# Two low rank products issued as a pair, and the state products of two heads alternated in two banks, in a two-layer hybrid decoder trunk

## The chip, the core and the metric

The kernel runs on one core of one Trainium2 chip. The metric is the device time of one execution in microseconds (us), median of several runs; lower is better. The program uses five engines with a queue of instructions each: TensorE (PE, with its weight loads as PEld), VectorE (DVE), ScalarE (ACT), GpSimd (POOL) and SyncE (SP, which issues most transfers). Products land in PSUM, which this kernel cuts into eight banks of 128 x 512 float32.

## What is computed

Two layers, 1024 tokens, width 1024, float32. Only layer 0's mixer and one function of layer 1 are touched by the change.

```python
# layer 0: y = concat(rwkv7(x), gla(x)) @ w_out ; layer 1: y = concat(s5(x), hgrn2(x)) @ w_out
# each layer: x = LN(alpha*x + mixer(x)); x = LN(alpha*x + hierarchical_moe(x))   (32 experts, top 2)
def rwkv7(p):                       # 8 heads of 64
    w = -softplus(-(w0 + tanh(wl) @ w2)) - 0.5      # low rank product 1: the decay
    a = sigmoid(a0 + al @ a2)                       # low rank product 2: the gate a
    kk = normalize(k * k_k)
    k = k * (1 + (a - 1) * k_a)
    S_t = S * exp(-exp(w)) + (S @ -kk) (kk * a)^T + v k^T ;  y_t = S_t r_t
    y = (groupnorm(y) + bonus) * (sigmoid(gl) @ g2) # low rank product 3
def gla(q, k, v, g):                # 4 heads, 64 x 128 states; hgrn2: 4 heads, 128 x 128
    o = q_decayed @ S_chunk  +  scores @ v          # a product with the state, one with the scores
```

## The kernel before

Everything is emitted by one Python program for the Tile framework; a scheduler then sets the order of each engine's queue. A queue runs in that order. What the scheduler may move is bounded by data and by buffers: a name such as `po` stands for a ring of PSUM banks (`RINGS`, line 654; `po` is the single bank f, `pp` the single bank e, `y` bank g, `ch` bank h, `iv` and `gs` the two banks c and d), and the users of a ring take it in the order in which the program text asks for it. A product into a ring of one bank waits until the last reader of the bank's former content, in the order of the text, is through.

Layer 0 (`layer0`, L1692) does two blocks of 512 tokens, n = 0 and 1. In each, `rwkv` (L282) runs four halves (`rwkv_half`, L314), one per pair of heads, pr = 0 to 3. For each half three projections are made (`proj_T`: L175, L176, L177, 24 products each into bank ring `pj`). Then `gla` (L607) makes its projections and runs `gla_core` (L512) twice, for two heads each. `gla` reuses buffers of `rwkv` by name.

One RWKV half is a long chain:

- the first low rank product (L328) and its sigmoid give the decay `cum`, `P`; the second (L340) and its sigmoid give `av`, from which DVE makes `k`, `av*kk` and the four parts of `BK` (L354 to L365);
- transposes of `BK` (L398), scores (L408), masks on DVE (L412 to L414);
- the inverse of a triangular matrix by doubling: nine groups of 16 small products (L425), each read by DVE (L433, L435, L440) before the next;
- a recurrence over 8 chunks: three products per chunk in ring `ch` (L447, L452, L458) with copies by ACT (L450, L454) and DVE (L453, L461) between them, and the output products (L466, L467);
- the tail: three products into `po` (group norm L471 and L475, third low rank product L482), then `y*p` on DVE (L483), the last reader of `po`.

Each half asks for `pp` and `po` in this order: `pp` for both low rank products and two more (L346, L369), `po` for the tail's three.

`gla_core` ends with the products of each head in turn: for each of four chunks one with the state (L571) and one with the scores (L572) into one bank of ring `y`, which before held the sums for the new states (L562), read by DVE (L566). Layer 1 calls `gla_core` with one head of 128 rows (`hgrn2_head`, L1303).

Of the kernel before, what the change touches and what calls it, by code (L numbers as in the profile page):

```python
# [35 lines left out]
class Kern:  # L36
# [38 lines left out]
    def store(self, dst, src):  # L75
        self.nc.gpsimd.dma_start(dst, src)
# [233 lines left out]
    def work(self, name, shape=(128, 512), bufs=1):  # L310
        tag, bufs = self.tags.get(name, (name, bufs))
        return self.place.get(tag, self.mpool).tile(list(shape), F32, tag=tag, bufs=bufs, name=name)

    def rwkv_half(self, pr, n, k, r_, v, wlal, sgl, ydram):  # L314
        nc, K, work = self.nc, self.rk, self.work
        C, lora = K["C"], K["lora"]
        cs = slice(pr * 128, (pr + 1) * 128)
# [3 lines left out]
        def col(i):  # L321
            return C[:, i + pr:i + pr + 1]

        def c8(x):
            return x.rearrange("p (c t) -> p c t", t=64)


        p = self.mm1(lora[0:64, 0, cs], wlal[0:64])  # L328
        sg = work("sg")
        self.sigmoid(sg, p, bias=col(14))  # L330
        cum = work("cum")
        nc.vector.tensor_tensor_scan(cum, self.cmask.rearrange("p c t -> p (c t)"), sg, 0.0, op0=OP.mult, op1=OP.add)
# [3 lines left out]
        nc.scalar.activation(iP, cum, AF.Exp, scale=EC)  # L336
        PC = work("PC", (128, 8), bufs=2)
        nc.gpsimd.tensor_copy(PC, c8(P)[:, :, 63])

        p = self.mm1(lora[64:128, 0, cs], wlal[64:128])  # L340
        av = work("av")
        self.sigmoid(av, p, bias=col(18))

        sq = work("tmp", bufs=2)
        nc.scalar.activation(sq, k, AF.Square, scale=col(22))
        p = self.mm1(self.blk, sq)  # L346
# [10 lines left out]
        Q, Zd = self.pairs[pr % 2]  # L357
        BK = work("BK", (128, 8, 2, 64))
        for h in range(2):
            r = H[h]  # L360
# [8 lines left out]
        p = self.mm1(self.blk, r_)  # L369
# [32 lines left out]
        for g in range(2):  # L402

            sc = [piv().rearrange("p (c x) t -> p c x t", x=2) for _ in H]
            for j in range(4):
                c = 4 * g + j
                for h, r in enumerate(H):
                    nc.tensor.matmul(sc[h][:, j], BK[r, c], Q[r, c, 2 * h:2 * h + 2, :], start=True, stop=True)  # L408
            for h, psc in enumerate(sc):
                r, rk = H[h], H[1 - h]  # L410
# [10 lines left out]
        def diag(lhs, rhs):  # L421
            p = piv()
            for j in range(8):
                for r in H:
                    nc.tensor.matmul(p[r, j, :], lhs[r, j, :], rhs[r, j, :], start=True, stop=True)  # L425
            return p
# [4 lines left out]
        for s in (2, 4, 8, 16, 32):  # L431
# [5 lines left out]
            else:  # L437
                p = diag(T1, Z)
# [5 lines left out]
        y = work("y")  # L444
        for c in range(8):
# [16 lines left out]
            if c % 4 == 3:  # L462
                py = self.bank("y", (128, 4, 2, 64))
                for j in range(4):
                    i = c - 3 + j
# [5 lines left out]
        p = self.mm1(self.blk, y, "po")  # L471
# [3 lines left out]
        p = self.mm1(self.blk, sq, "po")  # L475
# [6 lines left out]
        p = self.mm1(lora[:, 1, cs], sgl, "po")  # L482
# [29 lines left out]
    def gla_core(self, n, q, k, f, heads, S, norm_g, store):  # L512

        nc, work = self.nc, self.work


        SC = [work(f"gSC{i}", (128, 4, 128), bufs=2) for i in range(len(heads))]
        Q, Ke, D = work("gQ", bufs=2), work("gK", bufs=2), work("gD")
        nc.vector.tensor_tensor(Q, q, f, op=OP.mult)
        d, at = f, 0  # L520
        for s in (0, 1, 2, 4, 8, 16, 32, 64):
            L, R = (k if s < 2 else Ke), Q if s else q
            ps = [self.bank("gs", (128, 4, 128)) for _ in heads]
            if s:
                ps = [p.rearrange("p (h c) t -> p h (c t)", h=2)[:, 0].rearrange("p (c t) -> p c t", t=64) for p in ps]
            for c in range(4):
                cc = slice(128 * c, 128 * c + 128)
                for p, (r, _, _, _) in zip(ps, heads):
                    rhs = R[r, cc]
                    if s:  # L530
                        rhs = rhs.rearrange("p (b t) -> p b t", t=2 * s)[:, :, s:]
                    if s < 64:
                        nc.tensor.matmul(p[:, c, :], L[r, cc], rhs, start=True, stop=True)  # L533
                    else:
                        nc.tensor.matmul(p[0:64, c, :], L[r, 128 * c:128 * c + 64], rhs, start=True, stop=True)
            if s:
                nb = 256 // s
                b3 = lambda x: x.rearrange("p (b t) -> p b t", t=2 * s)
                d2 = d.rearrange("p (b h) -> p b h", h=2)
                bc = lambda h: d2[:, :, h:h + 1].to_broadcast([128, nb, s])  # L540
                if s == 1:
                    nc.gpsimd.tensor_copy(b3(Ke)[:, :, 1:], b3(k)[:, :, 1:])
                nc.vector.tensor_tensor(b3(Ke)[:, :, :s], b3(L)[:, :, :s], bc(1), op=OP.mult)
                nc.vector.tensor_tensor(b3(Q)[:, :, s:], b3(Q)[:, :, s:], bc(0), op=OP.mult)
                d = D[:, at:at + nb]
                at += nb
                nc.vector.tensor_tensor(d, d2[:, :, 0], d2[:, :, 1], op=OP.mult)
            for i, p in enumerate(ps):
                if s == 64:
                    nc.scalar.activation(SC[i][0:64, :, 64:], p[0:64], AF.Copy)  # L550
                elif s == 0:
                    nc.vector.tensor_tensor(SC[i], p, self.ident[:, None, :].to_broadcast([128, 4, 128]), op=OP.mult)
                else:
                    m = self.glev[s].rearrange("p (b t) -> p b t", t=s)[:, None].to_broadcast([128, 4, 64 // s, s])
                    nc.vector.copy_predicated(SC[i].rearrange("p c (b t) -> p c b t", t=2 * s)[:, :, :, s:], m,
                                              p.rearrange("p c (b t) -> p c b t", t=s))
        kdT = self.token_major(Ke, "gkdT")

        pS = self.bank("y", (128, 4, 128))
        for c in range(4):  # L560
            for r, V, _, _ in heads:
                nc.tensor.matmul(pS[r, c, :], kdT[:, c, r], V[:, c, :], start=True, stop=True)  # L562
        St = work("gS", (128, 4, 128), bufs=2)
        for c in range(4):
            src = S if c == 0 else St[:, c - 1, :]
            nc.vector.scalar_tensor_tensor(St[:, c, :], src, d[:, c:c + 1], pS[:, c, :], op0=OP.mult, op1=OP.add)  # L566
        for i, (r, V, gate, row) in enumerate(heads):
            po = self.bank("y", (128, 4, 128))
            for c in range(4):
                cc = slice(128 * c, 128 * c + 128)  # L570
                nc.tensor.matmul(po[:, c, :], S[r, :] if c == 0 else St[r, c - 1, :], Q[r, cc], start=True, stop=False)  # L571
                nc.tensor.matmul(po[:, c, :], V[:, c, :], SC[i][:, c, :], start=False, stop=True)  # L572
            o = work("go", bufs=2)
            nc.scalar.activation(o, po.rearrange("p c t -> p (c t)"), AF.Copy)
            sq = work("ptmp")
            nc.scalar.activation(sq, o, AF.Square)
            p = self.mm1(self.ones, sq, "po")
            nc.scalar.activation(sq, p, AF.Ln, scale=1.0 / 128, bias=self.eps)
            nc.scalar.activation(sq, sq, AF.Exp, scale=-0.5)
            nc.vector.scalar_tensor_tensor(o, o, norm_g, sq, op0=OP.mult, op1=OP.mult)  # L580
            store(row, o, gate)
        nc.gpsimd.tensor_copy(S, St[:, 3, :])
# [1211 lines left out]
```

## Time and profile before

| | |
|---|---|
| median of 3 runs | 2887.45 us (2884.76 to 2890.49) |
| the profiled execution's own time | 2887.3 us |
| its span | 2885.5 us |
| granted TensorE clock over the span | 0.951 of full |
| layer 0's mixer, first to last product | about 0 to 800 us of the span |
| layer 0's experts | about 900 to 1500 us |
| layer 1's mixer | about 1550 to 2150 us |
| layer 1's experts | about 2200 to 2830 us |

The profile is one execution. Its span leaves out 1.8 us of the execution's own time. A row of the timeline gives the start, the duration, the engine and the instruction (a product of float32 shows as two records, marked x2). A row of a table by stretch gives the busy time of each engine in it, with the number of instructions, then the granted clock, the share of the DMA engines, and GB/s.

### The profile page before, as it was taken

What the parts mean: (1) busy time and instruction counts of PE and PEld (TensorE: products, weight loads), DVE (VectorE), ACT (ScalarE), POOL (GpSimd) and SP (SyncE); (2) the same over time, 40 slices, a digit from 0 to 9 for tenths busy, and PEclk for the clock granted to TensorE, in tenths of its full rate; (3) what the DMA queues carried; (4) which work ended last, traced back from release to release, by engine and by line L of the source; (5) the groups of instructions that cost most, each with busy time, mean ns of one, the idle gap of its engine ahead of it and who ended that gap; (6) DMA issues with size and microseconds to landing.
All of it is one profiled execution on the core that took longest, in us unless ns stands there. A gap on an engine that the chain in (4) does not pass through costs nothing.

```text
span 2885.5 us, 41351 instructions
## 1 busy us (share of the span) xinstructions
PE 2670.9 (93%) x15348; PEld 1980.4 (69%) x15348; DVE 2100.3 (73%) x3228; ACT 1586.0 (55%) x2292; POOL 819.5 (28%) x991
## 2 busy tenths in 40 slices
PE   8999999999897999999988788789997999999994
PEld 6777776766685677777764667678776677777772
DVE  5775447764357899999967568886445899999985
ACT  4343333333333788888864333334533788888872
POOL 5333323323400211111105455462320111111104
PEclk9999989999897999999999889899898999999998
DMA  3111221101354999999967221122443999999985
GB/s 112 31 38 34 62 74 38 30 28 48 128 174 178 373 379 378 378 376 380 385 250 232 88 62 45 56 67 77 140 150 134 355 379 381 382 382 378 380 309 191
DMA packets 234644, 581.57 MB, mean 202 GB/s; under 512 B 48110, under 2 KB 156743, under 8 KB 185287
## 3 DMA queue, kind: packets, MB, share of 16 engines
q1 hardware_dynamic: 212294, 518.04, 50.1%
q0 software_dynamic: 22144, 60.85, 6.0%
q8 instruction: 122, 2.00, 0.3%
q14 instruction: 84, 0.68, 0.1%
HBM read 541.99 MB, written 52.43 MB: 206 GB/s over the span
## 4 chain that ended last, share of the span: by engine, by line
issue 36%; PE 32%; DVE 10%; POOL 8%; DMA 2%; ACT 2%; POOLq 0%; SPq 0%; DVEq 0%; ACTq 0%
POOL xg L970 4%; PE bpj L176 4%; PE bpj L177 4%; PE bpj L175 4%; PE bgs L533 3%; POOL ybuf L1034 2%; PE bpj L729 2%; PE bpj L730 2%; PE bpj L728 2%; PE biv L425 1%; PE bpp L785 1%; PE bpo L182 1%; PE biv L1220 1%; PE by L571 1%; PE by L572 1%
## 5 line engine op out<-in xcount | busy, mean ns | idle before, releaser
L111 DVE TENSOR_TENSOR mlo<-raw,mhi 128x1024 fp32r<-128x1024 f32 x768 | 921.8, 1222 | 105.4 <-ACT mhi L1058 71.2
L1058 ACT ACTIVATE mhi<-raw 128x1024 fp32r<-128x1024 f32 x768 | 806.4, 1059 | 204.5 <-PE bpo L1027 87.1
L118 POOL TENSOR_TENSOR wlo<-wraw,whi 128x256 fp32r<-128x256 f32 x368 | 282.4, 797 | 323.0 <-ACT whi L106 309.3
L175 PE MATMUL bpj<-hT_hi,whi 128*128 128x512 f32 x736 | 306.2, 416 | 12.7 <-DVE hq L588 11.8
L970 POOL DMA_INDIRECT xg<-hdram,gi x64 | 135.4, 2116 | 632.0 <-PE by L982 600.9
L177 PE MATMUL bpj<-hT_hi,wlo 128*128 128x512 f32 x736 | 305.1, 415 | 4.5 <-POOL wlo L118 4.5
L176 PE MATMUL bpj<-hT_lo,whi 128*128 128x512 f32 x736 | 306.4, 416 | 0.0
L996 PE MATMUL bpj<-mhi,xh 128*96 128x512 f32 x512 | 204.9, 400 | 0.0
L106 ACT ACTIVATE whi<-wraw 128x1024 fp32r<-128x1024 f32 x92 | 97.3, 1057 | 195.4 <-PE bpj L176 140.7
L998 PE MATMUL bpj<-mhi,xl 128*96 128x512 f32 x512 | 204.4, 399 | 0.1
L997 PE MATMUL bpj<-mlo,xh 128*96 128x512 f32 x512 | 204.0, 399 | 0.0
L996 PE MATMUL biv<-mhi,xh 128*96 128x512 f32 x512 | 201.8, 394 | 0.0
L997 PE MATMUL biv<-mlo,xh 128*96 128x512 f32 x512 | 201.6, 394 | 0.0
L998 PE MATMUL biv<-mhi,xl 128*96 128x512 f32 x512 | 201.6, 394 | 0.0
L175 PEld LDWEIGHTS bpj<-hT_hi,whi 128*128 128x128 f32 x736 | 142.5, 194 | 47.0 <-DVE hq L588 13.1
L1034 POOL DMA_INDIRECT ybuf<-yo,si x64 | 60.2, 940 | 385.1 <-ACT yo L1033 375.4
L177 PEld LDWEIGHTS bpj<-hT_hi,wlo 128*128 128x128 f32 x736 | 142.0, 193 | 34.8 <-POOL wlo L118 6.7
L176 PEld LDWEIGHTS bpj<-hT_lo,whi 128*128 128x128 f32 x736 | 142.0, 193 | 30.0 <-issue 3.8
L998 PEld LDWEIGHTS bpj<-mhi,xl 128*96 128x96 f32 x512 | 84.1, 164 | 38.0 <-DVE xl L111 1.4
L729 PE MATMUL bpj<-wol,oyh 128*128 128x512 f32 x256 | 105.8, 413 | 4.2 <-POOL wol L118 4.2
L997 PEld LDWEIGHTS bpj<-mlo,xh 128*96 128x96 f32 x512 | 84.2, 164 | 36.5 <-issue 0.2
L996 PEld LDWEIGHTS bpj<-mhi,xh 128*96 128x96 f32 x512 | 84.1, 164 | 35.9 <-issue 0.2
(617 smaller groups left out, 5686.7 us busy)
## 6 DMA issues: line engine op xcount, KB each, us to landing
raw<-in_moe_w_dram SPq DMA_DIRECT2D x384, 1024.0 KB
wraw<-in_ab_w_in_dram SPq DMA_DIRECT2D x50, 512.0 KB
wraw<-in_cd_w_in_dram SPq DMA_DIRECT2D x40, 512.0 KB
cy<-ybuf SPq DMA_DIRECT2D x16, 1024.0 KB
oyr<-ydram SPq DMA_DIRECT2D x16, 512.0 KB
hdram<-or POOLq DMA_DIRECT2D x16, 512.0 KB, 2.9
lnh<-hdram SPq DMA_DIRECT2D x16, 512.0 KB
ydram<-go POOLq DMA_DIRECT2D x16, 256.0 KB, 2.7
```

The lines of the kernel that those rows point to most:

```text
L111: self.keep(self.nc.vector.tensor_tensor(lo, src, hi.bitcast(F32), op=OP.subtract))
L118: lo_engine.tensor_tensor(lo[:, s], src[:, s], hi[:, s].bitcast(F32), op=OP.subtract)
L175: nc.tensor.matmul(dst, wh[:, k, :], xh[:, k, :], start=(k == 0), stop=False)
L176: nc.tensor.matmul(dst, wh[:, k, :], xl[:, k, :], start=False, stop=False)
L177: nc.tensor.matmul(dst, wl[:, k, :], xh[:, k, :], start=False, stop=(k == KT - 1))
L729: nc.tensor.matmul(p, yh[:, k, :], wl[:, ds_], start=False, stop=False)
L970: self.nc.gpsimd.indirect_dma_start(out=xg[:CAP, :], out_offset=None, in_=hdram, in_offset=bass.IndirectOffsetOnAxis(ap=gidx, axis=0), bou ...
L996: self.keep(self.nc.tensor.matmul(p, xh[:, k, :], wh, start=(k == 0), stop=False))
L997: self.keep(self.nc.tensor.matmul(p, xh[:, k, :], wl, start=False, stop=False))
L998: self.keep(self.nc.tensor.matmul(p, xl[:, k, :], wh, start=False, stop=(k == KT - 1)))
L1034: return nc.gpsimd.indirect_dma_start(out=ybuf, out_offset=bass.IndirectOffsetOnAxis(ap=sidx, axis=0), in_=y, in_offset=None, bounds_check ...
L1058: self.keep(self.nc.scalar.activation(hi, src, AF.Copy))
```

## The change

1. In `rwkv_half` the second low rank product is issued right after the first one, in the text, and lands in ring `po` in place of `pp`. Its sigmoid stays where it was.
2. In `gla_core` the products with the states come first, for both heads alternating by chunk, head 0 in ring `y` and head 1 in ring `ch`; the products with the scores follow head by head. The bank is opened once (start on the first chunk alone).

```diff
-        p = self.mm1(lora[0:64, 0, cs], wlal[0:64])
-        sg = work("sg")
+        p, pa = self.mm1(lora[0:64, 0, cs], wlal[0:64]), self.mm1(lora[64:128, 0, cs], wlal[64:128], "po")
+        sg, av = work("sg"), work("av")
         self.sigmoid(sg, p, bias=col(14))
...
-
-        p = self.mm1(lora[64:128, 0, cs], wlal[64:128])
-        av = work("av")
-        self.sigmoid(av, p, bias=col(18))
+        self.sigmoid(av, pa, bias=col(18))
...
-        for i, (r, V, gate, row) in enumerate(heads):
-            po = self.bank("y", (128, 4, 128))
+
+        pos = [self.bank(x, (128, 4, 128)) for x in ("y", "ch")[:len(heads)]]
+        for c in range(4):
+            for po, (r, _, _, _) in zip(pos, heads):
+                nc.tensor.matmul(po[:, c, :], S[r, :] if c == 0 else St[r, c - 1, :], Q[r, 128 * c:128 * c + 128], start=(c == 0), stop=False)
+        for i, (po, (r, V, gate, row)) in enumerate(zip(pos, heads)):
             for c in range(4):
-                cc = slice(128 * c, 128 * c + 128)
-                nc.tensor.matmul(po[:, c, :], S[r, :] if c == 0 else St[r, c - 1, :], Q[r, cc], start=True, stop=False)
-                nc.tensor.matmul(po[:, c, :], V[:, c, :], SC[i][:, c, :], start=False, stop=True)
+                nc.tensor.matmul(po[:, c, :], V[:, c, :], SC[i][:, c, :], start=False, stop=(c == 3))
```

What it does to the order of PE's queue, at three places. In these rows a b ahead of a ring's name marks its bank, and from L344 to L558 a line of the changed kernel is 3 less than the same line before.

The first place is PE around the end of the half pr = 1 and the start of pr = 2, first block. Before:

```order
L182 MATMUL bpo<-ptmp,blk 128x512
L425 MATMUL biv<-T_1387,Z 64x64 x16
L182 MATMUL bpp<-wlal,lora 128x512
L182 MATMUL bpo<-sgl,lora 128x512
L425 MATMUL biv<-X,M 64x64 x16
L175 MATMUL bpj<-hT_hi,whi 128x512
L176 MATMUL bpj<-hT_lo,whi 128x512
L177 MATMUL bpj<-hT_hi,wlo 128x512
L175 MATMUL bpj<-hT_hi,whi 128x512
L182 MATMUL bpp<-wlal,lora 128x512
```

And with the change:

```order
L182 MATMUL bpo<-y,blk 128x512
L182 MATMUL bpo<-ptmp,blk 128x512
L182 MATMUL bpo<-sgl,lora 128x512
L182 MATMUL bpo<-wlal,lora 128x512
L395 MATMUL biv<-ident,BK 128x64 x14
L182 MATMUL bpp<-r,blk 128x512
L395 MATMUL biv<-ident,BK 128x64 x2
L405 MATMUL biv<-Q_275,BK 128x128 x8
L182 MATMUL bpp<-wlal,lora 128x512
```

The rows before are the tail of pr = 0 (`bpo`), the inverse of pr = 1 (L425) and both low rank products of pr = 2 (`wlal,lora`). The rows after are the tail of pr = 1, then the second low rank product of pr = 2, its transposes (L395, before L398) and scores (L405, before L408), and the first low rank product of pr = 3. The second product of a half now stands behind the tail of the half ahead of it; in the half pr = 0 of each block alone the two stand side by side.

The second place is PE in the recurrence of pr = 1, first block, two chunks of the eight. Before:

```order
L447 MATMUL bch<-SV,Q_281 128x128
L425 MATMUL biv<-X,M 64x64 x8
L452 MATMUL bch<-G,Zd_282 128x64
L425 MATMUL biv<-X,M 64x64 x5
L175 MATMUL bpj<-hT_hi,whi 128x512
L176 MATMUL bpj<-hT_lo,whi 128x512
L177 MATMUL bpj<-hT_hi,wlo 128x512
L458 MATMUL bch<-UV,BT 128x128
L466 MATMUL by<-R_1267,UV 128x128
L467 MATMUL by<-Q_281,SV 128x128
L425 MATMUL biv<-T_1957,Z 64x64 x3
```

And with the change:

```order
L444 MATMUL bch<-SV,Q_281 128x128
L449 MATMUL bch<-G,Zd_282 128x64
L455 MATMUL bch<-UV,BT 128x128
L463 MATMUL by<-R_1267,UV 128x128
L464 MATMUL by<-Q_281,SV 128x128
L444 MATMUL bch<-SV,Q_281 128x128
L449 MATMUL bch<-G,Zd_282 128x64
L455 MATMUL bch<-UV,BT 128x128
```

Before, the next half's inverse and projections stand between the products of the recurrence. Now nothing does, from its fourth chunk to its end, and all through that of pr = 2.

The third place is PE at the end of `gla_core`, first block, first two heads. Before, head 0:

```order
L571 MATMUL by<-gQ,glS 128x128
L572 MATMUL by<-gSC_3190,gV 128x128
L571 MATMUL by<-gQ,gS 128x128
L572 MATMUL by<-gSC_3190,gV 128x128
L571 MATMUL by<-gQ,gS 128x128
L572 MATMUL by<-gSC_3190,gV 128x128
```

And with the change, both heads:

```order
L568 MATMUL bch<-gQ,gS 128x128
L571 MATMUL bch<-gSC_3191,gV 128x128 x2
L568 MATMUL by<-gQ,glS 128x128
L568 MATMUL by<-gQ,gS 128x128 x3
L571 MATMUL by<-gSC_3190,gV 128x128 x4
L571 MATMUL bch<-gSC_3191,gV 128x128 x2
```

The four state products of head 1 (`bch`) go ahead one by one, the last of them in the first row here, and those of head 0 (`by`) follow in one run, when bank g is free. The two heads do not alternate in the queue.

In layer 1 the only difference is that the four products with the state stand ahead of the four with the scores, in each of the eight calls; from layer 0's experts on all else stands as before.

## Rows read from the trace of the kernel before

**Rows 1.** The page, busy time of each engine, share of the span:
```profile
PE 2670.9 (93%) x15348; PEld 1980.4 (69%) x15348; DVE 2100.3 (73%) x3228; ACT 1586.0 (55%) x2292; POOL 819.5 (28%) x991
```

**Rows 2.** Busy time by stretch (columns: PE, PEld, DVE, ACT, POOL, clock, DMA):
```profile
143.00:306.00 163.00, 160.48 (x1509) 112.84 (x1508) 103.11 (x219) 62.62 (x147) 56.34 (x92) 1.00 0.13 38
306.00:366.00 60.00, 59.49 (x348) 44.41 (x347) 26.90 (x54) 20.19 (x33) 20.23 (x27) 0.97 0.22 67
...
527.00:691.00 164.00, 160.95 (x1526) 113.73 (x1524) 103.77 (x214) 64.53 (x150) 56.35 (x90) 1.00 0.12 35
```

**Rows 3.** Timeline of PE: second low rank product of pr 1; last tail products:
```profile
84.55 0.69 PE L182 MATMUL bpp<-wlal,lora 64*128 64x512 f32 x1
...
143.24 0.70 PE L182 MATMUL bpo<-sgl,lora 128*128 128x512 f32 x1
...
196.34 0.70 PE L182 MATMUL bpo<-sgl,lora 128*128 128x512 f32 x1
...
305.39 0.70 PE L182 MATMUL bpo<-sgl,lora 128*128 128x512 f32 x1
...
526.70 0.70 PE L182 MATMUL bpo<-sgl,lora 128*128 128x512 f32 x1
...
691.08 0.70 PE L182 MATMUL bpo<-sgl,lora 128*128 128x512 f32 x1 [0.38 <-ACT ptmp L477]
```

**Rows 4.** Timeline of DVE and ACT: last reader of po; from av to the inverse:
```profile
146.90 0.68 DVE L483 TENSOR_TENSOR y<-y,bpo 128x512 f32<-128x512 f32 x1
...
434.70 0.75 DVE L191 TENSOR_SCALAR av<-bpp,rwp 128x512 f32<-128x512 f32 x1 [0.35 <-PE bpp L182]
...
435.48 0.63 ACT L192 ACTIVATE av<-av 128x512 f32<-128x512 f32 x1 [0.45 <-DVE av L191]
...
448.85 0.69 DVE L365 TENSOR_TENSOR BK<-k,cum 64x512 f32<-64x512 f32 x1
...
462.60 0.70 DVE L430 STREAM_TRANSPOSE X<-Z 128x512 f32<-128x512 f32 x1
```

**Rows 5.** Timeline: one step of the inverse, PE to DVE to PE:
```profile
90.96 1.15 PE L425 MATMUL biv<-T,Z 64*64 64x64 f32 x32
...
92.40 0.68 DVE L435 TENSOR_TENSOR X<-X,biv 128x512 f32<-128x512 f32 x1
...
93.39 1.15 PE L425 MATMUL biv<-X,M 64*64 64x64 f32 x32
```

**Rows 6.** Timeline of PE: the recurrence, from one chunk's first product to the next's:
```profile
277.58 0.46 PE L447 MATMUL bch<-SV,Q 128*128 128x128 f32 x2
...
280.91 0.46 PE L447 MATMUL bch<-SV,Q 128*128 128x128 f32 x2
```

**Rows 7.** Timeline of PE: the recurrence's last output product, first product of the tail:
```profile
299.39 0.39 PE L467 MATMUL by<-Q,SV 128*128 128x128 f32 x2
...
300.64 1.12 PE L182 MATMUL bpo<-y,blk 128*128 128x512 f32 x2
```

**Rows 8.** A stretch, and the same 16 records (8 products) at either clock:
```profile
380.00:390.00 10.00, 8.85 (x51) 7.54 (x51) 6.69 (x14) 2.71 (x4) 4.42 (x6) 0.50 0.39 107
...
372.70 2.85 PE L533 MATMUL bgs<-gQ,gK 64*128 64x64 f32 x16 [0.33 <-DVE gQ L544]
...
327.83 1.11 PE L533 MATMUL bgs<-gQ,gK 64*128 64x64 f32 x16
```

**Rows 9.** Timeline of PE: state and score products in turn; state-like products of two heads alternating:
```profile
336.48 0.48 PE L571 MATMUL by<-gQ,glS 64*128 64x128 f32 x2
336.89 0.49 PE L572 MATMUL by<-gSC,gV 128*128 128x128 f32 x2
...
306.45 1.16 PE L533 MATMUL bgs<-gq,gk 64*128 64x128 f32 x14
```

**Rows 10.** Timeline of PE: two projection products, start to start:
```profile
43.87 0.39 PE L177 MATMUL bpj<-hT_hi,wlo 128*128 128x512 f32 x1
44.09 0.39 PE L175 MATMUL bpj<-hT_hi,whi 128*128 128x512 f32 x1
```

## The prediction

> **What bounds the kernel now.** I read the busy shares first, then the table by stretch, then PE's timeline of one RWKV half, and last the queue orders printed above. PE is busy for 93% of the span [rows 1]. In layer 0's mixer it is more than that: 160.48 of 163 us over the halves pr = 1 to 3 of the first block, 160.95 of 164 us in the second [rows 2]. DVE, the next, has a third of that time free. So layer 0's mixer is bound by PE, and it is so only because the halves overlap: the second low rank product of pr = 1 runs at 84.55 us, long before the tail of pr = 0 ends with its third product at 143.24 us [rows 3]. While one half's recurrence goes from engine to engine, PE works on the next half's inverse. From tail to tail a half takes (305.39 - 143.24) / 3 = 54.0 us in the first block and (691.08 - 526.70) / 3 = 54.8 us in the second [rows 3].
>
> **The change, part by part.** *The low rank pair.* The second product moves from ring pp to ring po. In the program's text the uses of po by the half ahead (its tail) come first, so the product must wait until that tail's last reader, y*p on DVE, is through. Behind it wait av, k, BK, the transposes, scores, inverse and recurrence of its own half. The order shows it: three tail products, then this one, then the transposes; and the recurrences of pr = 1 and 2 stand alone in the queue. Three of the four halves of a block thus become one serial chain from tail to tail. Its length, from rows:
>
> - third tail product to the end of y*p: 143.24 to 146.90 + 0.68, so 4.4 us [rows 3, 4];
> - the second low rank product: 1.2 us, as the tail's first product of the same width (1.12) and a handoff [rows 7];
> - from it to the end of BK: one DVE step of 0.75, three ACT steps of 0.63, seven DVE steps of at most 0.69, with handoffs about 7.6 us [rows 4];
> - end of BK (448.85 + 0.69) to the end of the transpose that opens the inverse (462.60 + 0.70): 13.8 us, some of it other halves' work; I take 13.0 [rows 4];
> - nine steps of the inverse at 93.39 - 90.96 = 2.43 us: 21.9 us, the last one's DVE work standing for the step to the recurrence [rows 5];
> - eight chunks at 280.91 - 277.58 = 3.33 us: 26.6 us [rows 6];
> - last output product to third tail product: 305.39 - 299.39 = 6.0 us [rows 3, 7].
>
> The sum is 80.7 us against 54.0 and 54.8: 26.7 and 25.9 us more per half, 80 and 78 us per block for its three halves.
>
> *The clock.* Where PE has few and small products the granted clock has fallen to half, 1.2 of 2.4 GHz: in 380 to 390 us it is 0.50, and the same 8 products take 2.85 us there against 1.11 [rows 8]. The bare recurrences offer PE three dependent products of about 0.46 us per 3.33 us [rows 6]. No row shows one at half clock. The bounds are nothing, and a doubling of every product on the chain. I take 6 us for pr = 1 (five bare chunks and the tail), 16 for pr = 2 (eight chunks, the bare steps of its inverse, its tail), and 4 for pr = 3, whose recurrence shares PE and DVE with the first gla_core: 26 us per block, about half of the upper bound, which I put at 52.
>
> *What comes back.* The first half of a block loses work that the order moves behind its tail: by count 64 inverse products (4 groups of 1.15 us), three products of 1.12 us and 32 transposes and scores (4 us at 1.11 per 8), and gains 23 projections at 0.22 us [rows 5, 7, 8, 10]: 6 us earlier. And the scheduler fills pr = 3 with the first gla_core: between its tail and the second gla_core stand 100 projections and no gK products, where before 144 projections and 63 such products filled 60 us at 99% PE [rows 2]. 44 projections are 10 us [rows 10]; 63 products at 1.11 per 8 and some switching 11 us [rows 8]; the transposes, a product of 1.12 us and the state products below the rest: 27 us. Per block: 80 + 26 - 6 - 27 = 73 and 78 + 26 - 6 - 27 = 71 us. Sum: 144 us.
>
> *The state products.* Before, a state product of 64 rows and a score product of 128 rows start 0.41 us apart, while 14 records (7 products) on the two halves of the rows, alternating, take 1.16 us in all [rows 9]. Alternated, 8 state products would cost 1.3 us in place of 3.3, and with the scores in runs the 16 products about 3.3 us in place of 6.7. The order does not alternate them: ring y still holds the sums for the states, so head 1 goes ahead alone and head 0 follows. What is left is fewer changes of shape, about 2 us a call; two calls are inside the 27 above, the two others give 4 us. The Trainium skill, in TensorEngine Tiling (Array Packing), section Tiling Modes, says that tiles of different rows run in parallel and that a change of the tiling mode drains the engine. Rows 9 agree with both. By that rule with full alternation in all four calls and all eight pairs this change would be a gain; that is a rival below.
>
> *Layer 1.* Here both products have 128 rows. Four state products run ahead of four score products, so up to three of the latter no longer cover DVE's state updates: at most 3 x 0.41 us [rows 9] in eight calls, 10 us, least 0. PE is not the bound there throughout; I take 2. The experts move as they are.
>
> **The sum.** 144 - 4 + 2 = 142 us, onto the profiled execution's own 2887.3 us (0.15 below the median): **3029 us**.
>
> **The rivals.**
> - *The clock stays up.* Full clock in the bare stretches takes off 2 x 26 us: 2977. For it: three products per chunk and projections between most inverse steps. Against: the half clock in 380 to 390 us, where PE was nominally busy for 8.85 of 10 us [rows 8].
> - *Half clock all through the serial halves,* and the first gla_core crowding pr = 3's recurrence: twice the surcharge, 52 us more, and half of the 27 us lost in both blocks, 27 more: 3108. The Trainium skill, in TensorE: Matmul & The Clock Gate, Part 1, says that a gate passes half of the clock's pulses or all by how busy PE has been; it is on the side of a low clock here, and the sum does not use it.
> - *Faster: PE stays the bound.* If po were free in time, or projections filled the waits, only the savings would stay: two pairs side by side at one product each (2 x 1.2 us) and 4 x 2 us: 2877; with all pairs and states overlapped, 8 x 1.2 + 4 x 3.4 = 23 us: 2864. It decides from the point where a serial half fits into 54 us, or where the projections at hand fill the rest. Against: the order has 24 projections, 5 us, in the whole period of pr = 2, and 80.7 is far from 54.
> - *The delay is hidden by other work,* say because DMA-bound stages after it absorb some: 2930. Little speaks for it; the stages after start from layer 0's last output.
>
> **How the numbers follow.** The forecast, 3029 with half of the clock's surcharge, has 0.64; full clock 0.15; half clock throughout 0.15; partly hidden 0.02; faster 0.03; no change 0.01. The range runs from 2972, a little under the full clock case, to 3090, into the low clock case, whose upper part is left out with the faster and hidden ones. Faster and slower mean by over 0.2% (5.8 us), about what a measurement of this kernel can tell. Slower has 0.64 + 0.15 + 0.15 + 0.02 = 0.96.
>
> **What would show it.** In the changed profile: the second low rank product of pr = 1 to 3 some 5 us behind the third tail product of the half ahead; 80 to 100 us from tail to tail for these halves; PE busy for about half of the period of pr = 2 and the clock at 0.5 in the bare recurrences; the second gla_core of the first block starting near 437 us in place of 366; stages after layer 0 of the same length. It is wrong if halves still overlap, if tail to tail stays under 65 us, or if the expert stages change.

## The result, and the profile after

The changed kernel takes **3040.27 us** (median of 4 runs, 3039.48 to 3041.52) against 2888.52 us (2884.76 to 2890.49) for the kernel before on the same chip: a ratio of 1.0522, 95% interval 1.051 to 1.0535. The forecast was 3029, slower. The profiled execution took 3041.52 us, 154.2 us more than that of before; its span is 3039.7 us, its mean granted clock 0.913 against 0.951.

The page of the changed kernel, the busy time of each engine and the slices of PE and its clock:

```profile
PE 2734.0 (90%) x15348; PEld 2023.8 (67%) x15348; DVE 2109.1 (69%) x3228; ACT 1583.4 (52%) x2292; POOL 807.6 (27%) x991
...
PE   8986899987899889999998887889999699999995
...
PEclk8977898986899889999999988989989799999997
```

and the same two rows of slices of the kernel before:

```profile
PE   8999999999897999999988788789997999999994
...
PEclk9999989999897999999999889899898999999998
```

The work is the same, the instruction counts too [rows 1]. PE's busy time has grown by 63 us, with not one product more: the same products at a lower clock. The slices that have fallen are in the first third, layer 0's mixer.

PE's timeline of the changed kernel shows where (start, duration, instruction, what ended the idle time before it):

```profile
135.77 1.13 PE L182 MATMUL bpo<-sgl,lora 128*128 128x512 f32 x2
140.13 1.12 PE L182 MATMUL bpo<-wlal,lora 64*128 64x512 f32 x2
...
226.75 2.08 PE L182 MATMUL bpo<-sgl,lora 128*128 128x512 f32 x2 [0.78 <-ACT ptmp L474]
230.23 2.07 PE L182 MATMUL bpo<-wlal,lora 64*128 64x512 f32 x2 [1.41 <-DVE y L480]
...
317.29 2.08 PE L182 MATMUL bpo<-sgl,lora 128*128 128x512 f32 x2 [0.78 <-ACT ptmp L474]
320.77 2.07 PE L182 MATMUL bpo<-wlal,lora 64*128 64x512 f32 x2 [1.41 <-DVE y L480]
...
406.76 1.02 PE L182 MATMUL bpo<-sgl,lora 128*128 128x512 f32 x2
...
439.61 1.16 PE L530 MATMUL bgs<-gq,gk 64*128 64x128 f32 x16
...
592.63 1.12 PE L182 MATMUL bpo<-sgl,lora 128*128 128x512 f32 x2
...
863.83 1.02 PE L182 MATMUL bpo<-sgl,lora 128*128 128x512 f32 x2
...
896.68 1.16 PE L530 MATMUL bgs<-gq,gk 64*128 64x128 f32 x16
```

Read the pairs. `sgl,lora` is the tail's third product of one half, `wlal,lora` into `bpo` the second low rank product of the next. Each follows the tail by 3.5 to 4.4 us, and the idle time before the second and third ends with `DVE y L480`: y*p, the last reader of `po`. Before, that product ran at 84.55 us for pr = 1, a whole tail ahead [rows 3]. From tail to tail it is now 91.0, 90.5 and 89.5 us, where it was 54.0 [rows 3]. `bgs<-gq,gk` opens the second `gla_core`: it stands 32.9 us behind the last tail in either block, where it was 60 and 57.6 us before.

The same by stretch (PE, PEld, DVE, ACT, POOL, clock, DMA share, GB/s):

```profile
136.00:227.00 91.00, 77.24 (x608) 53.59 (x608) 44.22 (x86) 25.28 (x56) 26.88 (x42) 0.81 0.12 33
227.00:317.00 90.00, 62.01 (x518) 42.51 (x518) 38.63 (x79) 19.20 (x48) 11.89 (x24) 0.67 0.03 10
317.00:407.00 90.00, 83.81 (x721) 61.17 (x722) 53.86 (x114) 29.21 (x65) 19.63 (x32) 0.93 0.12 33
407.00:440.00 33.00, 33.00 (x166) 24.72 (x166) 13.12 (x23) 12.74 (x20) 11.87 (x19) 1.00 0.27 89
```

Before, these halves had PE busy for 160.48 of 163 us at clock 1.00 [rows 2]. No engine is near its limit now in the period of pr = 2: PE 62 of 90 us (with products stretched by the clock), DVE 39. That is what a chain looks like.

### The profile page after: what moved, and what is told of

It is laid out like the page before. It is cut to its first block, busy times and chain, and to the rows that moved or that the text cites. A ratio compares the mean times of both kernels' runs of the same rounds, so it can differ in the third digit from the quotient of the medians.

```text
span 3039.7 us, 41356 instructions
## 1 busy us (share of the span) xinstructions
PE 2734.0 (90%) x15348; PEld 2023.8 (67%) x15348; DVE 2109.1 (69%) x3228; ACT 1583.4 (52%) x2292; POOL 807.6 (27%) x991
## 4 chain that ended last, share of the span: by engine, by line
issue 34%; PE 24%; DVE 8%; POOL 8%; ACT 2%; DMA 2%; POOLq 0%; SPq 0%; DVEq 0%; ACTq 0%
POOL xg L969 4%; PE bpj L175 2%; PE bpj L177 2%; PE bpj L176 2%; PE bgs L530 2%; POOL ybuf L1033 2%; PE bpj L728 2%; PE bpj L727 2%; PE bpj L729 2%; PE bpp L784 1%; POOL wol L118 1%; PE bpo L182 1%; PE biv L1219 1%; PE biv L422 1%; DVE sX L1588 1%
## 5 line engine op out<-in xcount | busy, mean ns | idle before, releaser
L530 PE MATMUL bgs<-gQ,gK 64*128 64x64 f32 (+1 forms) x640 | 87.3, 319 | 24.7 <-DVE gQ L541 23.8
```

## Experiments

**1. The low rank pair alone.** The diff is the first half of the change, as printed above (`pa` in ring `po`); `gla_core` is that of before.

> The kernel before with the low rank pair alone (second product early in the text, in ring po); gla_core as before. Theory A (the one bank of po makes three halves of each block serial): nearly all of the 152 us, 3025 to 3045 us; tails some 90 us apart; layer 1 as before. Rival B (the state products ahead of the score products cost a good part): under 2990 us.

Measured: 3049.88 us (3042.92 to 3050.8) against 2889.28; ratio 1.0547 [1.0517, 1.0578]. Its stretches from tail to tail read as those of the whole change:

```profile
136.00:227.00 91.00, 76.71 (x610) 52.69 (x609) 44.80 (x87) 25.72 (x56) 26.90 (x42) 0.83 0.12 33
227.00:318.00 91.00, 64.80 (x519) 45.08 (x518) 38.31 (x79) 19.29 (x48) 11.89 (x24) 0.61 0.03 10
```

The pair carries all of the loss. The time lies 5 us above the expected range, about what the states, which are missing here, gain in run 2.

**2. The state products alone.** The second half of the change, on the kernel before.

> The kernel before with the state products alone moved; low rank products as before. Theory A: 2880 to 2900 us, a few us gained in layer 0's two blocks by fewer changes of shape and some 4 us lost in layer 1, where no score product covers DVE's state updates. Rival B: 2920 us or more.

Measured: 2883.64 us (2880.81 to 2888.85); ratio 0.998 [0.9967, 0.9994]. A small gain, about 6 us. The first product of layer 0's experts starts 5.5 us earlier (914.9 against 920.4 us), though of a head's four products there only one stands beside one of the other head.

**3. The tail out of the pair's ring.** The changed kernel, with the ring conflict taken away and all else kept, the pair in `pp` and `po` included:

```diff
-        p = self.mm1(self.blk, y, "po")
+        p = self.mm1(self.blk, y, "y")
...
-        p = self.mm1(self.blk, sq, "po")
+        p = self.mm1(self.blk, sq, "y")
...
-        p = self.mm1(lora[:, 1, cs], sgl, "po")
+        p = self.mm1(lora[:, 1, cs], sgl, "y")
```

> The changed kernel with the three products of each half's tail in ring y (bank g) in place of po, so that po is free when the next half asks for it; the pair still side by side in pp and po. Theory A: the halves overlap again, tails 54 to 56 us apart, 2870 to 2895 us, pairs starting within 0.02 us of each other where they stand side by side. Rival C (not the ring but issuing both products together shapes the order): stays above 3000 us. Rival D (ring y then holds up the recurrence's output products): 2910 to 2980 us.

Measured: 2890.52 us (2888.51 to 2901.53); ratio 1.0002 [0.9987, 1.0016]. The loss is gone, but for some 5 us against run 4, which also has the gain of the states; where those go was not tried apart. PE's timeline of this kernel, pr = 1: the pair, and 54 us later the third product of the tail of pr = 0:

```profile
89.90 1.12 PE L182 MATMUL bpp<-wlal,lora 64*128 64x512 f32 x2
92.03 1.12 PE L182 MATMUL bpo<-wlal,lora 64*128 64x512 f32 x2
...
145.61 1.13 PE L182 MATMUL by<-sgl,lora 128*128 128x512 f32 x2
```

So it is not `po` as a bank, nor issuing the two products together, that costs 150 us, but standing behind the tail in the ring. Side by side the pair stands only for pr = 0; in the other halves the two start 2.1 us apart, as in the rows above.

**4. The pair issued together, both in `pp`.**

```diff
-        p, pa = self.mm1(lora[0:64, 0, cs], wlal[0:64]), self.mm1(lora[64:128, 0, cs], wlal[64:128], "po")
+        p, pa = self.mm1(lora[0:64, 0, cs], wlal[0:64]), self.mm1(lora[64:128, 0, cs], wlal[64:128])
```

> The changed kernel with the second low rank product issued together with the first in the text, but in ring pp as before. Theory A: the text's order costs nothing where the ring is the old one: 2880 to 2900 us, within 5 us of the kernel with the state products alone. Rival C: above 2930 us.

Measured: 2885.4 us (2882.67 to 2891.32); ratio 0.9985 [0.9972, 0.9999]. The place in the text costs nothing; what is left is the gain of the states.

**5. One half of four in `po`.** As 4, but the second product goes to `"po" if pr == 2 else "pp"`.

> The changed kernel, but of the four halves of a block only pr = 2 asks for its second low rank product in ring po; the other three ask for pp, so one half per block is put behind the tail of the half ahead, not three. Theory A (PE idles because the next half's inverse is not there to fill the recurrence): the serial half keeps its 81 to 90 us from tail to tail, but pr = 3, whose second product is in pp, may now fill its gaps with its own inverse and have a period of 30 to 45 us; so much less than a third of the loss per block remains: 2890 to 2935 us in all. Rival D (each half that waits for the ring costs a fixed 27 to 36 us, whoever stands beside it): 2 x 27 to 36 over 2885, 2939 to 2957 us.

Measured: 2917.52 us (2915.29 to 2917.66); ratio 1.0092 [1.0077, 1.0108], 32 us over 4. The total is theory A's, the way to it is not. The stretches tail to tail for pr = 2, for pr = 3, and on to the second `gla_core`:

```profile
192.00:282.00 90.00, 78.30 (x778) 56.20 (x777) 60.94 (x121) 29.14 (x65) 19.93 (x33) 0.92 0.09 28
282.00:338.00 56.00, 55.18 (x435) 40.69 (x435) 27.55 (x63) 19.82 (x46) 15.47 (x27) 0.91 0.12 34
338.00:382.00 44.00, 44.00 (x243) 33.05 (x241) 15.56 (x35) 15.95 (x26) 15.11 (x23) 1.00 0.25 79
```

The serial half still takes 90 us, though PE is busy for 78 of them: its gaps are filled, with the inverse of pr = 3 and products of `gla`. Yet pr = 3 does not shrink to 30 to 45 us; it takes 56. The time comes back behind it: from its tail to the second `gla_core` 43 us (337.52 to 380.47), where 4 takes 59 (305.10 to 363.93). Two serial halves cost 32 us, six cost 155: a serial half with a neighbour that may overlap it costs some 16 us, one in a row of three some 26.

**6. Dummy products in the bare recurrences.** The changed kernel, and for pr = 1 and 2 behind each of a chunk's three products:

```diff
+        pf, ones = (self.bank("po"), self.cmask.rearrange("p c t -> p (c t)")[:, 0:256]) if pr in (1, 2) else (None, None)
...
             nc.tensor.matmul(pg, Q[:, c, 1:3, :], SV[:, c], start=True, stop=True)
+            if pf is not None:
+                nc.tensor.matmul(pf[:, 0:256], SV[:, c], ones, start=True, stop=True)
...
```

> The changed kernel with 24 dummy products of 128x256 more in the recurrence of pr = 1 and of pr = 2 (one behind each of the three products of a chunk, into a bank of ring po that nobody reads; the output is untouched). Theory E (steps of the bare recurrence take 4.25 us in place of 3.33 because the clock is at half, and it is at half because PE has little to do): the granted clock stays near 1 in the bare recurrences, steps come back to 3.3 to 3.6 us, 13 bare steps per block and the half clock inverse of pr = 2 gain 12 to 25 us per block: 2990 to 3020 us. Rival F (the steps are longer because of the handoffs of ACT, DVE and POOL, or the dummies do not lift the clock): steps of 4.2 us or longer, as each dummy takes 0.56 us at full clock and 1.1 at half on the same engine: 3035 to 3080 us.

Measured: 3014.22 us (3013.13 to 3016.42); ratio 1.043 [1.0415, 1.0446], so 26 us faster than the change by adding work. Two recurrence steps of pr = 2 in the changed kernel:

```profile
293.01 0.77 PE L444 MATMUL bch<-SV,Q 128*128 128x128 f32 x2
297.27 0.77 PE L444 MATMUL bch<-SV,Q 128*128 128x128 f32 x2
301.53 0.77 PE L444 MATMUL bch<-SV,Q 128*128 128x128 f32 x2
```

and with the dummies:

```profile
287.02 0.46 PE L445 MATMUL bch<-SV,Q 128*128 128x128 f32 x2
290.69 0.46 PE L445 MATMUL bch<-SV,Q 128*128 128x128 f32 x2
294.09 0.46 PE L445 MATMUL bch<-SV,Q 128*128 128x128 f32 x2
297.48 0.46 PE L445 MATMUL bch<-SV,Q 128*128 128x128 f32 x2
```

A step falls from 4.26 us to 3.4, near the 3.33 of before [rows 6]. The stretch of the bare recurrence of pr = 2, six chunks and the tail up to its third product, first in the changed kernel:

```profile
284.50:317.20 32.70, 22.82 (x65) 15.13 (x64) 5.40 (x19) 6.73 (x24) 5.87 (x14) 0.50 0.00 1
```

then with the dummies:

```profile
280.20:306.70 26.50, 22.28 (x102) 13.40 (x100) 5.39 (x19) 6.74 (x24) 5.88 (x14) 0.96 0.00 1
```

PE gets through 65 records in 32.7 us at clock 0.50, or 102 in 26.5 us at 0.96; DVE and ACT do the same work in both. Theory E holds: with nothing but products added the clock stays up, and the steps are shorter. The Trainium skill, in TensorE: Matmul & The Clock Gate, Part 1, says that the gate follows how busy PE has been; the two stretches agree. The dummies are a probe, no cure: the conflict costs six times as much as they give back.

**7. Alternating for good, tail in `y`.** As 3, and in `gla_core` the first ring is `po`:

```diff
-        pos = [self.bank(x, (128, 4, 128)) for x in ("y", "ch")[:len(heads)]]
+        pos = [self.bank(x, (128, 4, 128)) for x in ("po", "ch")[:len(heads)]]
```

> The changed kernel with two edits: the tail's three products in ring y in place of po (2890.5 us alone), and the state products of head 0 in ring po in place of y, so that head 0 and head 1 can alternate in PE's queue. Theory G (the state products of two heads, 64 rows each on the two halves of the rows, run side by side once they alternate): 8 state products take 1.3 to 1.7 us in place of 3.3, four calls, where PE is the bound: 5 to 8 us under the tail in y alone, 2882 to 2886 us. Rival H (the calls are bound by DVE's new states or by projections that fill anyway): 2889 to 2892 us.

Measured: 2885.56 us (2880.58 to 2895.4); ratio 0.9985 [0.9975, 0.9995]. Its interval overlaps that of 3, whose runs were on another occasion; the expected size is there, but this run alone does not settle it.

**8. Alternating for good, pair in `pp`.** 4 with the edit of 7.

> The changed kernel with the second low rank product back in ring pp (2885.4 us alone), issued where the change has it in the text, and the state products of head 0 in ring po in place of y, so that the two heads can alternate in PE's queue. Theory G (state products of two heads run side by side once they alternate): 4 to 8 us under 2885.4, 2877 to 2881 us, which would beat the kernel before by 0.3% or more. Rival H: 2884 to 2887 us, and po, which the tail of pr = 3 uses, may hold up the first call: up to 2895 us.

Measured: 2881.06 us (2875.36 to 2883.76); ratio 0.9969 [0.9958, 0.998]. It beats the kernel before. The experts of layer 0 start 10 us earlier (910.3 against 920.4), but layer 1's mixer, from its first product with the state to the opening one of its last call, takes 417 us against 410, in one execution each.

**9 and 10. Alternating in layer 0 alone.** Rings `po` and `ch` and the state products ahead only where there are two heads; with one head the text of before. Run 9 on top of 4, run 10 on the kernel before.

```diff
+        if len(heads) == 2:
+            pos = [self.bank(x, (128, 4, 128)) for x in ("po", "ch")]
+            for c in range(4):
+                for po, (r, _, _, _) in zip(pos, heads):
+                    nc.tensor.matmul(po[:, c, :], S[r, :] if c == 0 else St[r, c - 1, :], Q[r, 128 * c:128 * c + 128], start=(c == 0), stop=False)
         for i, (r, V, gate, row) in enumerate(heads):
-            po = self.bank("y", (128, 4, 128))
+            po = pos[i] if len(heads) == 2 else self.bank("y", (128, 4, 128))
             for c in range(4):
...
+                if len(heads) == 1:
...
```

> Both low rank products in ring pp as in the run before, the state products of the two heads alternating in rings po and ch in layer 0, and layer 1's products with the state and the scores in turn in ring y, as in the kernel before. In the run with alternation in both layers the first gather product of the experts of layer 0 came 10 us earlier (910.3 against 920.4), but from the first to the last state product of layer 1 it took 417 us against 410. Theory I (layer 1's loss comes from its new order): layer 1 stays at 410 us, 2874 to 2878 us in all. Rival J (layer 1's length varies between programs whatever its own order, as in the low rank pair alone, where its order of products is the one of before and it took 413.4 us): 2877 to 2883 us, with 412 to 418 us there.

> The kernel before with one edit: the state products of the two heads alternate in rings po and ch in layer 0. Low rank products and layer 1 are as before. It prices the alternation that the change names but that its order does not give. Theory G: 8 state products side by side take 1.3 to 1.7 us in place of 3.3 and the scores run without changes of shape, four calls where PE is the bound: the experts of layer 0 start 6 to 12 us earlier than in the kernel before, and the time is 2877 to 2883 us. Rival H (nothing, since DVE's new states end the wait): within 2 us of the kernel before.

Measured: run 9 2878.82 us (2877.47 to 2882.7), ratio 0.9967 [0.9955, 0.9979]; run 10 2880.52 us (2878.02 to 2889.39), ratio 0.9976 [0.9967, 0.9984]. Theory G's size is there in run 10: the total falls by 8 us. The first products of layer 0's experts, in the kernel before and in run 10, 9.6 us earlier:

```profile
920.41 0.88 PE L982 MATMUL bch<-ident,xg 96*128 96x96 f32 x4 [6.01 <-DMA xg<-hdram,gi]
...
910.79 0.88 PE L987 MATMUL bch<-ident,xg 96*128 96x96 f32 x4 [6.04 <-DMA xg<-hdram,gi]
```

PE's timeline of run 10, second call of the first block, chunks 1 to 3 and the start of the score products:

```profile
394.21 0.37 PE L571 MATMUL bpo<-gQ,gS 64*128 64x128 f32 x1
394.22 0.37 PE L571 MATMUL bch<-gQ,gS 64*128 64x128 f32 x1
394.43 0.27 PE L571 MATMUL bpo<-gQ,gS 64*128 64x128 f32 x1
394.43 0.27 PE L571 MATMUL bch<-gQ,gS 64*128 64x128 f32 x1
394.54 0.27 PE L571 MATMUL bpo<-gQ,gS 64*128 64x128 f32 x1
394.54 0.27 PE L571 MATMUL bch<-gQ,gS 64*128 64x128 f32 x1
...
395.08 1.16 PE L577 MATMUL bpo<-gSC,gV 128*128 128x128 f32 x8
```

Each product shows as two records here, and the two heads start within 0.01 us of each other. Six state products take 0.87 us, 0.29 per pair, where in turn with the scores each took 0.41 [rows 9]. Not all of that comes from the pairing. In the changed kernel three products of one head run in a row without a partner, up to the first score product:

```profile
413.62 0.83 PE L568 MATMUL by<-gQ,gS 64*128 64x128 f32 x6
414.38 0.82 PE L571 MATMUL by<-gSC,gV 128*128 128x128 f32 x5
```

Three alone take 0.76 us, 0.25 each; three pairs take 0.87. So keeping products of one shape together brings 0.41 down to 0.25, and the second head then costs 0.11 us more for all three. The Trainium skill, in TensorEngine Tiling (Array Packing), section Tiling Modes, says that different tiles run in parallel; these rows agree. Runs 2 and 4, with the first saving and little of the pairing, start the experts 5.5 and 3.8 us earlier, runs 10 and 9 9.6 and 10.0; whether the rest is the pairing or the earlier free bank was not told apart.

Layer 1 keeps its old order in both runs and takes 412.4 and 412.7 us by the marks of run 8, as 413.4 in run 1, where it is untouched too, against 410.0 in the kernel before: rival J. These are single executions. In runs 2 and 3 and in the change PE's products stand in the same order there, but for two or three places among some 1000 groups. The opening products of the calls, with their first and last start, in run 3 and in the change:

```profile
L568 PE MATMUL by<-gQ,hgS x16: 271/276/582, 1683.8 to 2103.0; 128*128 128x128 f32 x16
...
L568 PE MATMUL by<-gQ,hgS x16: 273/276/582, 1833.3 to 2247.3; 128*128 128x128 f32 x16
```

That is 419.2 and 414.0 us (run 2: 412.9). So neither the 3 us nor the 417 of run 8 shows what an order of products costs there; that stays open. Runs 8, 9 and 10 are not told apart by their intervals; all three beat both kernels.

## Why the prediction was right

The direction, the cause and the size held, the size with some luck: errors in its terms cancelled. Point by point:

- **Three serial halves per block.** Expected 80 and 78 us, and 26 of clock, over the three periods of a block: 106 and 104. Measured, from the first to the last of the four tails: 271.0 against 162.2 us and 271.2 against 164.4, so 108.8 and 106.8 more. Runs 1, 3 and 4 show the cause.
- **The serial sum of 80.7 us** was for full clock. The links of pr = 2 in the changed trace, with mine in brackets: tail product to y*p 3.4 (4.4; its rows give 4.3), low rank product 2.2 (1.2), to the end of BK 7.2 (7.6), to the inverse 13.7 (13.0), inverse 25.1 (21.9), recurrence 31.1 (26.6), to the next third product 7.9 (6.0). Together 90.5. The inverse was counted one group short: ten groups of 16 products run, not nine, but each takes 2.2 us once the clock is up, not 2.43, so these two errors cancel (22.0 against 21.9). What the inverse has beyond that lies mostly in its first two steps, 3.2 and 3.9 us, the end of a stretch at clock 0.65 (226.8 to 260.0 us). Recurrence and tail are longer by the half clock, as 6 shows for the recurrence.
- **The clock's split was wrong, and its sum came near by luck.** 6, 16 and 4 us for pr = 1, 2, 3 were expected; over 80.7 the periods have 10.3, 9.8 and 8.8. For pr = 1 and 2 the dummies give back 6.4 us each (their periods are 84.6 and 84.1 us). No dummies stand in pr = 3, so they tell nothing of it. Most of its 8.8 us are not the clock's: its recurrence shares PE with the first `gla_core`, at full clock. These are its second and its last chunk, and the stretch around them:

```profile
371.38 0.49 PE L444 MATMUL bch<-SV,Q 128*128 128x128 f32 x2
...
397.64 0.49 PE L444 MATMUL bch<-SV,Q 128*128 128x128 f32 x2
...
360.00:406.80 46.80, 46.40 (x376) 35.57 (x375) 25.19 (x63) 16.46 (x44) 12.94 (x22) 1.00 0.09 24
```

  Six steps take 26.3 us, 4.4 each; against 3.33, eight chunks make 8.4 us. The price of 3.33 us was that of a quiet stretch: in the kernel before, too, the recurrence of pr = 2 takes 4.3 us a step beside other work (217.52 to 247.77, seven steps). The prediction had named this sharing, but as a rival and a part of its 4 us. The row of 2.85 us that it took for the half clock starts at 372.70, ahead of its stretch from 380; a row of the same length stands at 381.02. The rival with full clock all through, 2977, fell; so did half clock in all halves, 3108.
- **What comes back.** The recapture was put at 27 us per block: 27.2 and 24.7 measured (32.9 us in place of 60 and 57.6). The first half came 7.5 us earlier where 6 were expected; the terms named for it add up to 6.9. The second `gla_core` starts 74.2 us later in the first block (73 expected) and 148.0 in the second (144).
- **The other two calls of `gla_core`** were to give 4 us. From the second block's last `gla_core` to layer 0's experts the delay grows from 148.0 to 149.9 us; before its first tail it falls by 8.2, of which the first half's gain, 7.5 in the first block, leaves 0.8 for a call. Together the two calls give nothing, so this term was mis-sized by at least 4 us. Run 2 alone has 5.5 us for all four calls.
- **Layer 1** was to add 2 us; it and all behind it add 4.3 (154.2 less 149.9). Runs 1 and 10 have 3 us there with the order of before, and nearly one order has spread over 6 us (runs 2 and 3), so the order need not be the cause.
- **The faster rivals** fell with run 1. The 14 us that full alternation in all calls was to be worth (4 times 3.4) measured 8 in run 10. A state product waits for DVE's new states: in run 10's first call the first pair runs at 331.50 us and the next at 334.51, as DVE begins the state that it reads at 333.73.
- **A sign that was misread in advance.** PE was to be busy for about half of the period of pr = 2. It shows 62 of 90 us, since products at half clock last longer; the idle time is less than the lost work.

## What to carry to other kernels

Where a bank or buffer is handed out in the order of the program text, a product at the head of the next iteration must not share it with one at the tail of this one: the overlap of the two is gone, and here that cost 5% of the whole kernel, while the same pair in another ring costs nothing. Look in the order for what stands behind the moved product, count the chain it opens, and look for the work of the stages around it that moves into its gaps, since 67.6 of the 215.6 us that the chains added came back that way. An order that should alternate has to be free to: as long as one of two banks is held by an earlier reader, only the text alternates. Part of the gain comes without it: with products of one shape kept together the experts of layer 0 start 4 to 5 us earlier, and with a free bank as well 10.

## What the runs showed of the hardware

- Adding 24 dummy products to each of two recurrences per block made the kernel 26 us faster: the granted clock was 0.96 in place of 0.50 over the recurrence and tail of pr = 2, and a step of three dependent products and the copies between them fell from 4.26 to 3.4 us.
- At half clock a busy share misleads: 22.82 of 32.7 us busy for 65 records, against 22.28 of 26.5 us for 102.
- Products of 64 rows: 0.41 us each in turn with products of 128 rows, 0.25 in a row of their own, and 0.29 per pair on the two halves of the rows. The gain in place is less than that of the products, as they wait for DVE.
- The stretch of layer 1's mixer took 412.9, 414.0 and 419.2 us in single executions of three programs whose products there stand in the same order but for two or three places.
